# Seven block products for eight in half the contraction of two projection groups

## The chip, the cores and the metric

The kernel runs on one core of a Trainium2 chip. The metric is the device time of one execution in microseconds. TensorE (PE in the profile) multiplies, VectorE (DVE), ScalarE (ACT) and GpSimd (POOL) do the rest, SyncE (SP) and POOL issue the transfers.

## The reference

One step of a hybrid decoder layer: 512 prompt tokens and 8 sample tokens, width 2048. One input projection of the layer input is cut by columns into groups. Three branches run on them: an mLSTM with 4 heads of width 256 (groups mq, mk, mv, output gate mo), a causal depthwise convolution of width 31 on 512 channels with a LayerNorm behind it (cu, cg), and sliding-window attention with 8 query heads (aq, ak, av). Each branch is multiplied by a SiLU gate of its own (mz, cz, az); the results are put side by side and go through an output projection, a residual and a LayerNorm.

```python
mq, mk, mv, mo, mi, mf, mz, cu, cg, cz, aq, ak, av, az = in_projection(x, w_in)
...
m_out = hn * jax.nn.sigmoid(mo.astype(f32)) * jax.nn.silu(mz.astype(f32))
c_out, new_buf = conformer_conv(cu, cg, conv_buf, conv_w, conv_b, conv_ln_g, conv_ln_b)
merged = jnp.concatenate([m_out.astype(x.dtype),
                          (c_out * jax.nn.silu(cz)).astype(x.dtype),
                          (a_out * jax.nn.silu(az)).astype(x.dtype)], axis=-1)
y = jnp.einsum('bte,ed->btd', merged, w_out)
```

## The kernel before

**Tiles of the projection.** The 520 tokens (512 and 8) stand in the free dimension, cut into two halves of 260 columns (`HS`, `hf` 0 and 1). The contraction of 2048 is 16 blocks of 128 (`k`). `ORDER` lists 62 output tiles of 128 columns: ak, av, four aq, for each head two mq, mk and mv, then cg and cu in turn, eight mo, eight mz, four az, four cz. The main loop goes over them; `e` is the number of a tile.

**Split numbers.** Each 32-bit operand is held as a high part in TensorE's format and a low part, the rest. `split` makes them: a cast on ScalarE (line 137) and a subtraction on VectorE (line 138). `mm3` multiplies high by high, low by high and high by low, three matmuls (lines 195 to 197). So one output tile has 16 x 2 x 3 = 96 matmuls of 128x260. The input x is split once and stays (`xh`, `xl`).

**Weights.** A tile's weights come as two halves of 1024 columns, 8 blocks each, in the order of `stream`. `w_load` issues the transfers on SP into one of `NRAW` raw buffers, `w_split` splits them into one of three buffer pairs (`whi`, `wlo`), most of a tile ahead of their use.

**The other work.** Convolution, attention and mLSTM are generators in a queue. After every 24 matmuls (a quarter of a tile, one tick) `pump` gives the queue a budget of credits (`BUDGET` 1.8 up to cg, `BUDGET2` 1.6 from there) and lets the first two generators run until the credits are spent; a step that yields `WAIT` goes on one tick later. `drain` runs a generator to its end. The instructions of TensorE, VectorE and ScalarE run in the order in which the program writes them; those of SP and POOL are ordered by the scheduler of the tile framework. `conv_taps` does 31 taps on VectorE for each of 4 channel blocks, `conv_norm` normalises by token blocks: `fwd` transposes on TensorE, takes statistics and subtracts on VectorE with a power on POOL in between, `bwd` transposes back two ticks later.

**After a tile.** `post_gate` (lines 802 to 805) activates the gate on ScalarE and multiplies it into the merged branch on VectorE. When a merged block is complete, `turn` splits it for the output projection: turns 0 to 7 write into L tiles, 8 to 15 into x tiles. `TURNED` says after which quarter of the cz tiles each is done.

**Buffers.** L, M and S tiles of 1072, 520 and 264 columns come from pools of `NL` 14, `NM` 13 and `NS` 17. A tile takes whichever buffer of its pool is free. In the attention (`att_prompt`), L tiles hold the keys, the queries, the values, the scores of a unit (`scores`) and the two probability tiles of a unit (`flip`); `values` multiplies these one tick after `flip`. PSUM has two pools, 3 banks for the accumulators (`acc_bank`) and 5 for all else (`bank`).

**The end.** Behind the loop, the scale, the bias and the residual are loaded through SP (lines 1040 to 1070). The output projection takes tokens 256 to 519 by output tiles of 128, and `flip_out` adds the residual; then it takes tokens 0 to 255.

## Time and profile before

| what | value |
|---|---|
| median of 3 runs | 1007.62 us (1007.06 to 1007.88) |
| profiled execution | 1005.27 us |
| its span, first to last instruction | 1003.5 us |
| mean granted TensorE clock | 0.997 |
| TensorE busy | 990.5 us |
| VectorE busy | 652.6 us |
| ScalarE busy | 385.4 us |
| POOL busy | 132.8 us |

The time holds the span and some 2 us around it. Busy times are of the profiled execution. TensorE's are pipelined, so that a busy TensorE may be one that waits for its data.

### The profile page before, as it was taken

The page shows a single profiled execution, that of the slowest core. Times are in us where ns is not written, and L with a number is a line of the kernel's source. Part 1 is how long each engine was busy: PE and PEld are TensorE (multiplying, and loading weights), DVE is VectorE, ACT ScalarE, POOL GpSimd, SP SyncE. Part 2 cuts the span into 40 slices and gives each one's busy share as a digit, 9 for nine tenths or more (in the row PEclk, how much of TensorE's full clock was granted, in tenths as well). Part 3 has the DMA queues.
Part 4 walks back from the last instruction along what each step waited for, and adds up shares of the span by engine and source line. Part 5 has one row for each costly group of instructions (what it writes and reads, how often), then busy time and mean ns, then how long its engine had stood idle before and what let it go on. Part 6 is the DMA issues. An engine that isn't in the chain of part 4 may idle for free.

```text
span 1003.5 us, 19258 instructions
## 1 busy us (share of the span) xinstructions
PE 990.5 (99%) x7911; PEld 971.1 (97%) x7911; DVE 652.6 (65%) x1308; ACT 385.4 (38%) x709; POOL 132.8 (13%) x225
## 2 busy tenths in 40 slices
PE   9999999999999999999999999999999999999995
PEld 9999999999999999999999999999999999998885
DVE  6465677567657646765667777778654455558866
ACT  6453454334344334434442222222244443433530
POOL 0010001222222232323311000000000000001102
PEclk9999999999999999999999999999999999999998
DMA  9222214466456436545543323323235585556842
GB/s 333 99 73 97 64 64 131 135 217 192 121 169 188 147 107 221 178 128 154 181 153 102 104 90 104 91 85 102 94 93 169 164 297 170 178 180 205 266 139 84
DMA packets 45976, 147.25 MB, mean 147 GB/s; under 512 B 6749, under 2 KB 8165, under 8 KB 45888
## 3 DMA queue, kind: packets, MB, share of 16 engines
q1 hardware_dynamic: 33840, 110.45, 33.8%
q0 software_dynamic: 11616, 35.03, 11.6%
q8 instruction: 62, 1.02, 0.4%
q10 hardware_dynamic: 432, 0.53, 0.2%
q14 instruction: 26, 0.21, 0.1%
HBM read 130.43 MB, written 15.56 MB: 145 GB/s over the span
## 4 chain that ended last, share of the span: by engine, by line
PE 94%; DVE 3%; ACT 1%; issue 1%; DMA 0%; POOL 0%; SPq 0%; POOLq 0%; DVEq 0%
PE mm L195 27%; PE mm L196 27%; PE mm L197 27%; PE bg L197 2%; PE bg L195 2%; PE bg L196 2%; PE bg L868 1%; PE bg L670 1%; PE bg L484 1%; PE bg L625 0%; DMA wr<-in_w_in 0%; DVE L L427 0%; PE bg L460 0%; PE bg L461 0%; ACT wh L137 0%
## 5 line engine op out<-in xcount | busy, mean ns | idle before, releaser
L195 PE MATMUL mm<-xh,wh 128*128 128x260 f32 (+1 forms) x2096 | 598.1, 285 | 0.5 <-ACT xh L137 0.3
L197 PE MATMUL mm<-xl,wh 128*128 128x260 f32 (+1 forms) x2096 | 592.8, 283 | 0.0
L196 PE MATMUL mm<-xh,wl 128*128 128x260 f32 (+1 forms) x2096 | 592.6, 283 | 0.0
L195 PEld LDWEIGHTS mm<-xh,wh 128*128 128x128 f32 x2096 | 396.0, 189 | 1.8 <-ACT xh L137 0.7
L196 PEld LDWEIGHTS mm<-xh,wl 128*128 128x128 f32 x2096 | 395.4, 189 | 0.7 <-DVE wl L138 0.4
L197 PEld LDWEIGHTS mm<-xl,wh 128*128 128x128 f32 x2096 | 394.8, 188 | 0.0
L138 DVE TENSOR_TENSOR wl<-wr,wh 128x1024 fp32r<-128x1024 f32 (+2 forms) x187 | 225.0, 1205 | 119.1 <-ACT wh L137 116.8
L137 ACT CAST wh<-wr 128x1024 fp32r<-128x1024 f32 (+2 forms) x187 | 193.6, 1035 | 213.3 <-PE mm L197 135.2
L333 DVE SCALAR_TENSOR_TENSOR L<-L,cst 128x512 f32<-128x512 f32 x120 | 90.0, 750 | 2.7
L208 POOL TENSOR_TENSOR T<-T,mhalf 128x1 f32<-128x1 f32 (+1 forms) x30 | 19.3, 645 | 319.5 <-DVE T L206 319.4
L804 ACT ACTIVATE S<-mm 128x260 f32<-128x260 f32 x48 | 18.6, 387 | 97.3 <-PE mm L197 97.3
L805 DVE TENSOR_TENSOR L<-L,S 128x260 f32<-128x260 f32 x48 | 20.6, 430 | 50.3 <-ACT S L804 50.3
L602 ACT ACTIVATE L<-mm 128x260 f32<-128x260 f32 x48 | 18.5, 385 | 64.8 <-PE mm L197 64.5
L195 PE MATMUL mm<-L,wh 128*128 128x264 f32 x128 | 36.4, 285 | 0.0
L196 PE MATMUL mm<-L,wl 128*128 128x264 f32 x128 | 36.4, 284 | 0.0
L197 PE MATMUL mm<-L,wh 128*128 128x264 f32 x128 | 36.3, 284 | 0.0
L777 DVE SCALAR_TENSOR_TENSOR M<-M,T,M 128x256 f32<-128x256 f32 x64 | 30.7, 480 | 6.7 <-ACT M L774 6.7
L780 DVE CUSTOM_DVE_ANT_0 S<-M,M 128x256 f32<-128x256 f32 x64 | 27.2, 425 | 2.2
L783 POOL DMA_DIRECT2D out_Cs<-M x28 | 15.6, 558 | 92.4 <-issue 63.9
L195 PEld LDWEIGHTS mm<-L,wh 128*128 128x128 f32 x128 | 24.1, 188 | 0.0
L197 PEld LDWEIGHTS mm<-L,wh 128*128 128x128 f32 x128 | 24.1, 188 | 0.0
L196 PEld LDWEIGHTS mm<-L,wl 128*128 128x128 f32 x128 | 24.1, 188 | 0.0
(353 smaller groups left out, 1133.1 us busy)
## 6 DMA issues: line engine op xcount, KB each, us to landing
wr<-in_w_in SPq DMA_DIRECT2D x122, 512.0 KB, 3.4
wr<-in_w_out SPq DMA_DIRECT2D x60, 512.0 KB, 3.6
M<-in_C POOLq DMA_DIRECT2D x32, 256.0 KB, 4.5
M<-qkD POOLq DMA_DIRECT2D x32, 256.0 KB, 5.0
out_Cs<-M POOLq DMA_DIRECT2D x32, 256.0 KB, 2.4
M<-in_xT SPq DMA_DIRECT2D x14, 260.0 KB, 6.2
M<-rowsD POOLq DMA_DIRECT2D x8, 260.0 KB, 4.6
M<-in_xp SPq DMA_DIRECT2D x8, 256.0 KB, 5.6
```

Source lines behind the costliest of these rows:

```text
L137: S.copy(out=hi, in_=raw)
L138: V.tensor_tensor(out=lo, in0=raw, in1=hi.bitcast(F32), op=ALU.subtract)
L195: PE.matmul(out, lhsT=wh, rhs=h, start=start, stop=False)
L196: PE.matmul(out, lhsT=wl, rhs=h, start=False, stop=False)
L197: PE.matmul(out, lhsT=wh, rhs=l, start=False, stop=stop)
L208: G.tensor_tensor(out=out, in0=out, in1=mhalf[:rows].broadcast_to([rows, n]) if n > 1 else mhalf[:rows], op=ALU.pow)
L333: V.scalar_tensor_tensor(out=y[:, 0:T], in0=t[:, k:k + T], scalar=cw[:, j, k:k + 1], in1=y[:, 0:T], op0=ALU.mult, op1=ALU.add)
L602: S.mul(out=hT[name, h][:, e, HS[hf]], in_=ps[:, 0:HALF], mul=1.0 / 16.0 if name == "mk" else 1.0)
L777: V.scalar_tensor_tensor(out=ce, in0=qkb[:, DK:2 * DK], scalar=gvv[:, e, b:b + 1], in1=ce, op0=ALU.mult, op1=ALU.add)
L780: V.tensor_tensor_reduce(out=junk, in0=ce, in1=qkb[:, 0:DK], scale=1.0, scalar=0.0, op0=ALU.mult, op1=ALU.add, accum_out=hc[:, e, b:b + 1])
L804: S.activation(out=s, in_=ps[:, 0:HALF], func=func)
L805: V.tensor_tensor(out=dst[:, HS[hf]], in0=dst[:, HS[hf]], in1=s, op=ALU.mult)
```

## The change

The eight tiles az and cz are taken in pairs. For blocks 0 to 7 of the contraction, a pair's product is seen as a 2x2 matrix product: two output tiles, two halves of the tokens, two halves of the eight blocks. It is computed with seven block products (Winograd's form of Strassen's algorithm) from sums of x blocks and sums of weight blocks. Blocks 8 to 15 are multiplied as before. A pair is written out by hand in eleven sections of 12 or 24 matmuls (`pair_up`). In detail:

- `x_sums` loads the quarters of x again through POOL, three tiles before the zone, makes four sums for each of four `j` and splits three; `x_sums_last` splits the fourth into the place of x blocks that are no longer wanted. Twelve M tiles hold the results.
- `prep` loads and splits the weights of a pair in six steps: `a` with the four weight sums behind it, `s12`, `s34`, `a'`, half of `b`, `b'`. `a` and `s12` of the next pair are made in sections 7 and 8.
- The seven products are combined on VectorE (`add`); the last combination and gate of a pair (`last`) stand in section 0 of the next one.
- The queue gets `BUDGET3` 1.2 after sections 1, 3, 5 and 7 to 10, `BUDGET2` is 1.8. `TURNED2` places the turns.
- The weights of az and cz are loaded in the order of the pairs. `NL` is 13, `NS` 13. Scale, bias and the residual of tokens 256 to 511 are loaded through POOL.

```diff
-BUDGET, BUDGET2 = 1.8, 1.6
+BUDGET, BUDGET2, BUDGET3 = 1.8, 1.8, 1.2
-NL, NM, NS, NRAW = 14, 13, 17, 3
+NL, NM, NS, NRAW = 13, 13, 13, 3
...
+SUMS = 3
+ZONE_AT = ("az", 0)
...
-TURNED = {(_i // 4, _i // 2 % 2, _i % 2): (_i - 1,) for _i in range(1, 9)}
-TURNED.update({(3, 0, 1): (8, 9, 10, 11), (3, 1, 0): (12, 13, 14), (3, 1, 1): (15,)})
 CONV0 = ORDER.index(("cg", 0))
+ZONE = ORDER.index(ZONE_AT)
+TURNED2 = {("cz", 0): {2: (0,), 4: (1,), 6: (2,), 7: (3,), 8: (4,), 9: (5,), 10: (6,)},
+           ("cz", 2): {1: (7,), 7: (8, 9, 10, 11), 9: (12, 13, 14), 10: (15,)}}
...
-    stream += [A["w_in"][e, hf] for e in range(2, NE) for hf in range(2)]
+    stream += [A["w_in"][e, hf] for e in range(2, ZONE) for hf in range(2)]
+    stream += [A["w_in"][e + a, hf] for e in range(ZONE, NE, 2) for hf in range(2) for a in range(2)]
...
             submit(("m", i // 2), m_prompt(i // 2))
             submit(("m", i // 2), m_sample(i // 2))
+    NJ = 4
+    sums = {}
+    xn1, xt2, xn3, xn4 = ([None] * NJ for _ in range(4))
+    def x_sums():
+        for j in range(NJ):
+            q = [sml()[:, 0:HALF] for _ in range(4)]
+            for i in range(4):
+                G.dma_start(out=q[i], in_=A["xT"][j + NJ * (i // 2)][:, HS[i % 2]])
+            x11, x12, x21, x22 = q
+            yield 0.0
+            yield WAIT
+            V.tensor_tensor(out=x11, in0=x11, in1=x12, op=ALU.subtract)
+            V.tensor_tensor(out=x12, in0=x12, in1=x22, op=ALU.subtract)
+            V.tensor_tensor(out=x22, in0=x22, in1=x11, op=ALU.add)
+            V.tensor_tensor(out=x21, in0=x21, in1=x22, op=ALU.subtract)
+            sums[j] = x11
+            yield 1.6
+            for dst, src in ((xt2, x22), (xn3, x12), (xn4, x21)):
+                t = mid(F32R)
+                dst[j] = t[:, HS[0]], t[:, HS[1]]
+                split(*dst[j], src)
+            yield 1.3
+    def x_sums_last():
+        for j in range(NJ):
+            xn1[j] = xh[j][:, HS[1]], xl[j][:, HS[1]]
+            split(*xn1[j], sums[j])
+    def w_pair():
+        return (wp.tile([P, 8 * P], F32R, tag="whi", bufs=3, name=nm("wh")),
+                wp.tile([P, 8 * P], F32R, tag="wlo", bufs=3, name=nm("wl")))
+    HW = (slice(0, NJ * P), slice(NJ * P, 2 * NJ * P))
+    wz, rz = {}, {}
+    def prep(q, what):
+        if q >= 2 * NE:
+            w_split(q + (1 if what == "a" else 2 if what == "s12" else 0))
+            return
+        w_load(q + 2)
+        t = None
+        if what == "a":
+            a, b = raws.pop(q), raws[q + 1]
+            t = wz[what] = w_pair()
+            split(*t, a)
+            u, v = (wp.tile([P, 8 * P], F32, tag="wsum", bufs=2, name=nm("ws")) for _ in range(2))
+            for out, x, y in ((u[:, HW[1]], b[:, HW[0]], b[:, HW[1]]), (u[:, HW[0]], u[:, HW[1]], a[:, HW[0]]),
+                              (v[:, HW[0]], a[:, HW[0]], b[:, HW[0]]), (v[:, HW[1]], u[:, HW[0]], a[:, HW[1]])):
+                V.tensor_tensor(out=out, in0=x, in1=y, op=ALU.add)
+            rz["s12"], rz["s34"] = u, v
+            w_load(q + 4)
+        elif what in ("s12", "s34"):
+            t = wz[what] = w_pair()
+            split(*t, rz.pop(what))
+        elif what == "b":
+            t = wz[what] = w_pair()
+            split(t[0][:, HW[0]], t[1][:, HW[0]], raws.pop(q + 1)[:, HW[1]])
+            w_load(q + 6)
+        else:
+            t = wz[what] = w_pair()
+            split(*t, raws.pop(q + (2 if what == "a'" else 3)))
+            w_load(q + (5 if what == "a'" else 7))
+            pos[1] = q + 4
+    def gate(src, name, i, hf):
+        dst = merged({"cz": 0, "az": 4, "mz": 8, "mo": 8}[name] + i)
+        s = sml()[:, 0:HALF]
+        S.activation(out=s, in_=src, func=AF.Sigmoid if name == "mo" else AF.Silu)
+        V.tensor_tensor(out=dst[:, HS[hf]], in0=dst[:, HS[hf]], in1=s, op=ALU.mult)
+    def pair_up(e, late):
+        q = 2 * e
+        na, nb = ORDER[e], ORDER[e + 1]
+        before(*na)
+        before(*nb)
+        p1, p6, p5, p7, c11, c12, c21, c22 = (f()[:, 0:HALF] for f in (
+            acc_bank, acc_bank, acc_bank, bank, bank, acc_bank, acc_bank, acc_bank))
+        s1, u2, u3, u4 = (sml()[:, 0:HALF] for _ in range(4))
+        x0 = [(xh[j][:, HS[0]], xl[j][:, HS[0]]) for j in range(2 * NJ)]
+        x22 = [(xh[j][:, HS[1]], xl[j][:, HS[1]]) for j in range(NJ, 2 * NJ)]
+        def times(out, what, off, xs, start, stop):
+            wh, wl = wz[what]
+            for j in range(NJ):
+                ks = slice((off + j) * P, (off + j + 1) * P)
+                mm3(out, wh[:, ks], wl[:, ks], *xs[j], start and j == 0, stop and j == NJ - 1)
+        def rest(out, what, hf, start):
+            wh, wl = wz[what]
+            for k in range(8, NK):
+                ks = slice((k - 8) * P, (k - 7) * P)
+                mm3(out, wh[:, ks], wl[:, ks], xh[k][:, HS[hf]], xl[k][:, HS[hf]], start and k == 8, k == NK - 1)
+        def add(out, x, y, op=ALU.add):
+            V.tensor_tensor(out=out, in0=x, in1=y, op=op)
+        def sec0():
+            times(p1, "a", 0, x0[:NJ], True, True)
+            if late:
+                late.pop()()
+            prep(q, "s34")
+            S.copy(out=s1, in_=p1)
+        def sec1():
+            times(p6, "s12", 0, xt2, True, True)
+            add(u2, s1, p6, ALU.subtract)
+        def sec2():
+            times(p5, "s12", NJ, xn1, True, True)
+            add(u4, u2, p5)
+            prep(q, "a'")
+        def sec3():
+            times(c11, "a", NJ, x0[NJ:], True, False)
+            prep(q, "b")
+        def sec4():
+            times(p7, "s34", 0, xn3, True, True)
+            add(u3, u2, p7, ALU.subtract)
+            add(u2, u4, p7, ALU.subtract)
+        def sec5():
+            times(c12, "s34", NJ, x22, True, False)
+        def sec6():
+            times(c21, "b", 0, xn4, True, False)
+            prep(q, "b'")
+        def sec7():
+            rest(c11, "a'", 0, False)
+            add(s1, s1, c11)
+            gate(s1, *na, 0)
+            prep(q + 4, "a")
+        def sec8():
+            rest(c12, "a'", 1, False)
+            add(u4, u4, c12)
+            gate(u4, *na, 1)
+            prep(q + 4, "s12")
+        def sec9():
+            rest(c21, "b'", 0, False)
+            add(u3, c21, u3, ALU.subtract)
+            gate(u3, *nb, 0)
+        def last():
+            add(u2, c22, u2, ALU.subtract)
+            gate(u2, *nb, 1)
+        def sec10():
+            rest(c22, "b'", 1, True)
+            if e + 2 < NE:
+                late.append(last)
+            else:
+                last()
+        for i, sec in enumerate((sec0, sec1, sec2, sec3, sec4, sec5, sec6, sec7, sec8, sec9, sec10)):
+            sec()
+            if i in (1, 3, 5) or i > 6:
+                pump(BUDGET3)
+            for k in TURNED2.get(na, {}).get(i, ()):
+                turn(k)
     with tc.manual_schedule(engines=MAN):
-        for e in range(2, NE):
+        for e in range(2, ZONE):
             name, i = ORDER[e]
-            w_split(2 * e + 3)
+            if e == ZONE - SUMS:
+                queue.insert(0, ["x", x_sums(), 0])
+            if e == ZONE - 1:
+                drain("x")
+                prep(2 * ZONE, "a")
+            else:
+                w_split(2 * e + 3)
             budget = BUDGET if e < CONV0 else BUDGET2
             before(name, i)
             ps = [None, None]
             for half in range(2):
                 wh, wl = parts[2 * e + half]
-                if half == 1:
+                if half == 1 and e == ZONE - 1:
+                    prep(2 * ZONE, "s12")
+                    x_sums_last()
+                elif half == 1:
                     w_split(2 * e + 4)
                 for hf in range(2):
                     if half == 0:
                         if hf == 1:
                             after(name, i)
                     pump(budget)
-                    if name == "cz":
-                        for k in TURNED.get((i, half, hf), ()):
-                            turn(k)
+        late = []
+        for e in range(ZONE, NE, 2):
+            pair_up(e, late)
     lng, lnb = [big(), big()], [big(), big()]
     for i in range(2):
         for t, n in ((lng, "lng"), (lnb, "lnb")):
-            SP.dma_start(out=t[i][:, 0:1024], in_=A[n][:, i * 1024:(i + 1) * 1024].partition_broadcast(P))
+            G.dma_start(out=t[i][:, 0:1024], in_=A[n][:, i * 1024:(i + 1) * 1024].partition_broadcast(P))
     def norm_out(tiles, sts, acc, n_st):
         mv = tiny()
     rr = [[mid()[:, 0:512] for _ in range(4)] for _ in range(2)]
     for q4 in range(4):
         for a in range(2):
-            SP.dma_start(out=rr[a][q4], in_=A["xp"][c0 + a * P:c0 + (a + 1) * P, q4 * 512:(q4 + 1) * 512])
+            G.dma_start(out=rr[a][q4], in_=A["xp"][c0 + a * P:c0 + (a + 1) * P, q4 * 512:(q4 + 1) * 512])
```

## Rows read from the trace of the kernel before

**Rows 1.** The page, part 1: engine, busy us, share of the span, instructions.
```profile
PE 990.5 (99%) x7911; PEld 971.1 (97%) x7911; DVE 652.6 (65%) x1308; ACT 385.4 (38%) x709; POOL 132.8 (13%) x225
```

**Rows 2.** The waits of TensorE, whole span: us in total, times, longest.
```profile
PE warm L112 <- DVE S L109: 1.1, 1, 1.1
PE mm L195 <- ACT xh L137: 0.3, 1, 0.3
PE mm L195 <- DVE L L427: 0.2, 1, 0.2
```

**Rows 3.** Windows ahead of and in the changed stretch: busy us (instructions), clock, DMA.
```profile
640.00:708.10 68.10, 68.10 (x571) 68.10 (x571) 54.46 (x76) 16.04 (x23) 0.89 (x1) 1.00 0.32 96
708.10:804.40 96.30, 96.30 (x810) 96.05 (x809) 50.98 (x77) 37.19 (x67) 2.73 (x5) 1.00 0.41 129
```

**Rows 4.** Timeline of ScalarE, gates of mz7 and cz3: start, us, [idle before].
```profile
708.32 0.39 ACT L804 ACTIVATE S<-mm 128x260 f32<-128x260 f32 x1 [2.48 <-PE mm L197]
...
804.67 0.39 ACT L804 ACTIVATE S<-mm 128x260 f32<-128x260 f32 x1 [0.90 <-PE mm L197]
```

**Rows 5.** Timeline of VectorE from 639 to 800 us.
```profile
639.86 0.43 DVE L805 TENSOR_TENSOR L<-L,S 128x260 f32<-128x260 f32 x1 [0.98 <-ACT S L804]
640.21 1.53 DVE L333 SCALAR_TENSOR_TENSOR L<-L,cst 128x512 f32<-128x512 f32 x2
641.66 1.22 DVE L138 TENSOR_TENSOR wl<-wr,wh 128x1024 fp32r<-128x1024 f32 x1
642.79 3.11 DVE L333 SCALAR_TENSOR_TENSOR L<-L,cst 128x512 f32<-128x512 f32 x4
...
761.25 0.70 DVE L138 TENSOR_TENSOR L<-L,L 128x520 fp32r<-128x520 f32 x1
...
796.96 2.53 DVE L138 TENSOR_TENSOR xl<-L,xh 128x520 fp32r<-128x520 f32 x4 [1.19 <-ACT xh L137]
```

**Rows 6.** Timeline of ScalarE, a cast of weights and one of a turn.
```profile
708.60 1.05 ACT L137 CAST wh<-wr 128x1024 fp32r<-128x1024 f32 x1
...
767.65 0.62 ACT L137 CAST L<-L 128x520 fp32r<-128x520 f32 x1
```

**Rows 7.** Timeline of VectorE: the last tap, the first normalising step.
```profile
717.70 0.75 DVE L333 SCALAR_TENSOR_TENSOR L<-L,cst 128x512 f32<-128x512 f32 x1
...
723.11 0.70 DVE L203 BATCH_NORM_STATS2 T<-bg 128x6 f32<-128x512 f32 x1 [0.73 <-PE bg L348]
...
724.89 0.81 DVE L355 TENSOR_SCALAR M<-bg,T 128x512 f32<-128x512 f32 x1 [0.68 <-POOL T L208]
```

**Rows 8.** Attention: a wait of POOL; VectorE's scores and scaling; TensorE's value matmul, transposes.
```profile
POOL L L523 <- PE bg L461: 92.9, 1, 92.9
...
131.83 1.28 DVE L462 TENSOR_TENSOR L<-bg,S 128x512 f32<-128x512 f32 x2
137.42 1.23 DVE L476 TENSOR_TENSOR L<-L,T 128x1024 f32<-128x1024 f32 x1
...
134.30 0.39 PE L497 MATMUL bg<-L,L 128*128 128x512 f32 x1
140.73 1.03 PE L484 MATMUL bg<-ident,L 128*128 128x128 f32 x8
```

**Rows 9.** Windows at the end, behind the last matmul; the granted clock is third from last.
```profile
994.00:996.00 2.00, 0.00 (x0) 0.00 (x0) 1.54 (x4) 1.18 (x2) 0.98 (x2) 1.00 0.00 0
996.00:998.00 2.00, 0.00 (x0) 0.00 (x0) 1.97 (x3) 0.63 (x2) 1.92 (x2) 0.61 0.34 131
998.00:1000.00 2.00, 0.00 (x0) 0.00 (x0) 1.93 (x4) 0.00 (x0) 0.37 (x1) 0.50 0.38 138
```

**Rows 10.** Transfers: an issue on SP's queue; a kind of load with its us to landing.
```profile
780.51 0.33 SPq L1043 DMA_DIRECT2D L<-in_lng  x1
...
M<-in_xT ACTq DMA_DIRECT2D x2, 130.0 KB, 2.6
```

## Prediction

> **What bounds the kernel now.** I read the page first. TensorE is busy for 990.5 us of a span of 1003.5, VectorE for 652.6 [rows 1]. A busy TensorE may still be waiting inside its work, so the list of its waits came next: three, 1.6 us in all, at the start [rows 2]. The windows say the same of the stretch that is changed and of the one before it: PE fills both, and VectorE has 51.0 of 96.3 us of work where the change goes, 54.5 of 68.1 ahead of it [rows 3]. So time is won only by fewer matmuls, and every wait that another engine puts into TensorE's stream is paid in full. The zone (az, cz) runs from 708.1 to 804.4: its ends are the gate activations of mz7 and cz3 [rows 4].
>
> **What is removed.** A tile has 16 x 2 x 3 = 96 matmuls, a pair of tiles 192. In the new pair, sections 0 to 6 have 12 each and sections 7 to 10 have 24 each: 180. Four pairs save 48. The tiles ahead of the zone hold 571 matmuls in 68.10 us, 0.1193 us each [rows 3], so the saving is 48 x 0.1193 = 5.7 us. It is sure, because nothing hides TensorE.
> A rule weighed against this: the Trainium skill's page TensorE: Matmul & The Clock Gate, section Back-to-back issue gap, gives columns / 2.4 + 2.5 ns, which for 260 columns is 110.8 ns, an estimate, and a saving of 5.3 us in place of 5.7. The row decides.
>
> **What is added to VectorE and ScalarE.** Durations, alone or in a queue of their own kind: a 1024-column subtract 1.22 (1.13 from start to start), a 520-column one 0.70 (0.61), a 260-column operation 0.43 (0.35), a convolution tap 0.78 [rows 5]; on ScalarE a 1024-column cast 1.05, a 520-column one 0.62, a gate 0.39 [rows 4, 6]. The operations on 512 columns of weights are not in the trace; I take the 520-column row. Per pair VectorE gets 5.5 splits (6.8 us), four weight sums (2.4), eight combinations (3.4) and four gates (1.7): 14.3 us in a pair of 180 x 0.1193 = 21.5. A bare pair fits, but each result is wanted soon, since a section lasts only 1.43 or 2.87 us. The tight place is the passage from one pair to the next. Counted from the end of section 7, VectorE does a gate (done at 1.5), the split of the next pair's first weights (3.3), the four sums (5.6), the next gate (7.0) and the split of the two-block sums (8.6); TensorE wants those after three long sections and a short one, at 10.1. Work of over 1 to 1.5 us put between them becomes a wait of TensorE, and three things are put there.
>
> **First, the entry.** I counted the queue's credits through both programs. For the old one this puts the last tap into the third quarter of az0 and the first normalising step one quarter later, as the trace has it [rows 7]. For the new one, at 1.8, the x sums take places from mz5 on, the last ones are forced at the start of mz7, taps still fill mz7, and the last is in section 1 of az0. From the gate of mz6's second half (done on ScalarE 0.6 us into mz7) VectorE has in its queue: gates 3 x 0.35, eight x sums 2.8, six x splits 2.1, the first weights' split 1.13, four weight sums 2.44, ten taps 7.3, the sums' split 1.13, four splits of the last x sum 1.4: 19.3 us, while mz7 lasts 11.5. It is 8.5 us behind when the zone starts. Section 1 wants the low part of the sums at 1.55 and gets it at 2.8: 1.3 us of wait. Section 4 wants the low part of the third weights at 5.9 + 1.3 and gets it at 9.8: 2.6 us more. Entry: 3.9 us.
>
> **Second, the normalising steps of the convolution.** One forward step takes VectorE 2.6 us with its trip to POOL (723.11 to 725.70) [rows 7]; its back transposes stand on TensorE two pump places later. In the old zone the places were 2.87 us apart on a quiet VectorE. By the credits the new program has forward steps in az0 at sections 5 and 9, in az2 at 1, 5 and 8, the last back step at section 10. Counted from the end of section 7 of az2, VectorE reaches the sums' split at 8.6 as above and ends the forward step behind it at 11.2; TensorE gets to the back transposes after section 8, eight transposes (1.0) and sections 9 and 10, at 9.6: 1.6 us. Section 1 of az2 has the same with 0.8, and section 6 waits 0.2 for a split behind such a step. Together 2.6 us.
>
> **Third, the turns.** cz0 now has four turns in sections 7 to 10, 0.61 us each: 2.4 us in the passage to cz2, which had 0.9 free where the last combination must leave its PSUM bank for section 2. 1.6 us of wait. In the zone: 3.9 + 2.6 + 1.6 = 8.1 us.
>
> **Fourth, one L tile less, far ahead of the zone.** From attention unit 4 on, the keys (2), queries (4), values (1), merged halves (2), mLSTM inputs (2, later 3), two probability tiles and the new score tile make 14. That none is free the trace shows: POOL, idle, could not load the cached keys into an L tile until the last score matmul [rows 8]. With 13 the score tile has to wait for the first probability tile, which the value matmuls free one section later: the addition that ran at 131.83 can start at 134.30 + 0.39 = 134.7, 2.9 us late. Behind it on VectorE stand the maximum, the sums and the scaling (137.42 + 1.23 = 138.65), and the transposes at 140.73 wait for them [rows 8]: 2.1 us are spare, 0.8 us stalls. Three such units (4, 5, 6): 2.5 us. From below: 0, if the freed tile is not the one that VectorE waits for; from above 2.9 x 3 = 8.7, if the spare time is used otherwise.
>
> **Costed at nothing.** S tiles 17 to 13: I count nine alive at most in the old program, and in the new one some eleven with the x quarters. The budget of 1.8 ahead of the zone: VectorE has 54.5 of 68.1 us there [rows 3], one more half microsecond per tick stays under it, and parts are split most of a tile early. The 16 quarter loads of x on POOL: POOL has under 1 us of work from 640 to 708 [rows 3], such a load lands in 2.6 us [rows 10]; without that cover VectorE is later by as much, once. The scale, bias and residual loads moved from SP to POOL: SP issued the first at 780.5 [rows 10]; they now pass no weight load. They wait for M tiles that the x sums hold until section 6 of the last pair, and the first flip wants them two and a half output tiles after the zone, some 14 us. If late, VectorE stops there and with it the weight splits, some 3 us.
>
> **The sum.** -5.7 + 8.1 + 2.5 = +4.9 us. The profiled execution took 1005.27 us, 1.8 us more than its span; it would take 1010.2. The median of the runs, 1007.62, is 2.4 us above that execution, and the same sum gives **1012.5 us**. About 2 us, 0.2%, is what the measurement can tell from no change.
>
> **The rivals.**
> A. Attention is not touched, because the allocator finds another tile: the zone alone, -5.7 + 8.1, 1010.0. For it: the count of 14 rests on lifetimes that the trace shows only through POOL's wait.
> B. Faster: VectorE keeps up. If its short operations in a queue cost 10% less than I take them for, the entry leaves 1.8, the normalising 1.1 and the turns 0.7: 3.6 us of waits, and with attention untouched -5.7 + 3.6 = -2.1; with only the turns left -4.1, that is 1003.5 to 1005.5. It decides where the waits of zone and attention stay together under 3.7 us. Against it: the durations are rows, and 19.3 us of queue in a tile of 11.5 leave no room.
> C. VectorE falls further behind (the quarter loads, late flips, 5% dearer operations: 10.6 us in the zone): -5.7 + 10.6 + 2.5 + 3, 1018.
> D. The pauses lower TensorE's clock. After the last matmul the granted clock is still 1.00 two to four microseconds on, then 0.61 and 0.50 [rows 9]; my longest pause is 2.6 us. If it fell once, two short sections at half clock cost about 3 us: 1015.5. The Trainium skill's page TensorE: Matmul & The Clock Gate, section Why this matters for your kernels, speaks against the change here: it warns of idle gaps between bursts of matmuls, which bring the half clock back. By that rule, the trace agrees only for a pause longer than those I expect.
> E. Nothing to be measured: waits of 4 to 7.5 us in all, 1005.9 to 1009.4.
>
> **How the numbers follow.** Forecast 0.42, A 0.20, B 0.20, C 0.08, D 0.04, E 0.06. A stands at +2.4, just over the bound, so I give 0.12 of it to slower and 0.08 to same. Slower: 0.42 + 0.12 + 0.08 + 0.04 = 0.66; same 0.14; faster 0.20. The range leaves out the faster half of B and most of C: 1004 to 1017. The likeliest case by itself, with the attention term from 1 to 4 and 6 to 9.5 us in the zone, is 1009 to 1015.5.
>
> **What would show it.** PE's list of waits has new entries: in az0 on the subtract of a split, in az2 at the transposes of the convolution, at the start of cz2 on a combination, and near 131 to 165 us on the scaling of the scores. The count of 128x260 matmuls falls by 48 and the zone gets longer than 96.3 us all the same. The forecast is wrong if PE shows waits under 4 us in all, or if 130 to 170 us passes without one.

## The result, and the profile after

| | before | after |
|---|---|---|
| median of 4 runs | 1007.52 us (1007.06 to 1007.88) | 1018.75 us (1018.07 to 1022.06) |
| profiled execution | 1005.27 us | 1018.33 us |
| its span | 1003.5 us | 1016.5 us |

The change makes the kernel slower: ratio 1.0118, interval 1.0096 to 1.0141. The forecast was 1012.5, slower, with a range that ended at 1017. The direction was right, and the loss is more than twice the one forecast: 11.2 us by the medians, 13.0 by the spans of the profiled executions (that of the kernel before took 2 us less than the runs of this table; run 5 below, beside other runs of the old kernel, gives 13.4 by the medians).

Part 1 of the new kernel's profile page answers to [rows 1]: VectorE has 40 us more work, TensorE 1.3 us less, in a span that is 13.0 us longer.

```profile
PE 989.2 (97%) x7863; PEld 967.1 (95%) x7863; DVE 692.5 (68%) x1396; ACT 400.4 (39%) x739; POOL 145.9 (14%) x253
```

The list of TensorE's waits over the whole span answers to [rows 2] (us in total, times, longest):

```profile
PE mm L203 <- ACT xh L144: 3.3, 2, 1.7
PE mm L204 <- DVE wl L145: 2.3, 1, 2.3
PE bg L204 <- DVE wl L145: 2.3, 1, 2.3
PE bg L372 <- DVE M L363: 2.3, 2, 1.6
PE bg L492 <- DVE L L484: 1.6, 2, 0.8
PE mm L203 <- DVE S L1122: 1.2, 2, 0.9
...
PE bg L492 <- ACT wh L144: 0.8, 1, 0.8
...
PE mm L205 <- DVE xl L145: 0.2, 1, 0.2
```

Nearly every entry that the forecast named is there. The two waits on the low part `wl` are sections 1 and 4 of az0 (L203 to L205 are the lines of `mm3`, L145 the subtract of `split`). The two on `M` are back transposes of the convolution. The two on L1122, the line of `add`, are sections 1 and 2 of cz2. The three at L492 are the flips of attention; one of them is listed under a cast of weights, which ends at the same moment as the scaling (142.07). One entry was not named: of the two waits on the cast `xh`, one is at the start of the program, and the other, 1.7 us, lies behind the zone.

How much TensorE lost is not in that list. It is read from the number of matmuls that it does in a stretch. These windows of the kernel before cover the start and attention (busy us of PE with its instructions, then PEld, DVE, ACT, POOL):

```profile
0.00:130.00 130.00, 128.39 (x1035) 126.95 (x1036) 77.36 (x153) 67.56 (x144) 6.63 (x19) 1.00 0.38 129
130.00:190.00 60.00, 60.00 (x489) 59.11 (x488) 42.08 (x88) 28.56 (x73) 7.96 (x12) 1.00 0.41 127
```

The same of the new kernel, then its zone, whose 100.7 us answer to the 96.30 of [rows 3], and the entry of the output projection:

```profile
0.00:130.00 130.00, 127.05 (x1030) 125.88 (x1031) 76.53 (x153) 67.24 (x144) 6.62 (x19) 1.00 0.38 129
130.00:190.00 60.00, 57.36 (x460) 55.46 (x459) 40.97 (x87) 27.22 (x71) 7.96 (x12) 1.00 0.37 115
712.20:812.90 100.70, 92.58 (x762) 90.84 (x761) 77.04 (x133) 43.50 (x81) 8.64 (x16) 1.00 0.37 121
...
820.00:822.00 2.00, 1.52 (x7) 1.31 (x8) 0.70 (x1) 0.74 (x4) 0.00 (x0) 0.80 0.89 229
822.00:824.00 2.00, 2.00 (x11) 2.00 (x10) 1.12 (x1) 0.85 (x1) 0.00 (x0) 0.50 0.93 261
824.00:826.00 2.00, 2.00 (x16) 2.00 (x15) 0.11 (x1) 0.09 (x1) 0.00 (x0) 0.85 0.98 348
```

In the 60 us of attention 29 matmuls are missing, 3.5 us at 0.12 each, where PE shows 2.64 us of idle time. The zone has 48 matmuls fewer than before and lasts 4.4 us longer. Behind it TensorE pauses from 818.6 to 820.3, and then the granted clock falls from 1.00 to 0.50: 11 matmuls pass in a window that holds 19 at full clock (shown below for run 8).

Two markers tell how late the new kernel is behind that. The first is the first matmul of the output projection, with 264 columns, on TensorE's timeline; the second is ScalarE's copy of the second output tile, which waits for TensorE. Before:

```profile
804.47 0.29 PE L195 MATMUL mm<-L,wh 128*128 128x264 f32 x1
```

```profile
816.35 0.37 ACT L1151 COPY S<-mm 128x256 f32<-128x256 f32 x1 [1.88 <-PE mm L197]
```

After:

```profile
812.91 0.30 PE L203 MATMUL mm<-L,wh 128*128 128x264 f32 x1
```

```profile
828.78 0.37 ACT L1339 COPY S<-mm 128x256 f32<-128x256 f32 x1 [1.82 <-PE mm L205]
```

So the delay is 0.6 us after the first 130 us (five matmuls), 4.1 after attention, 8.4 at the end of the zone, 12.4 after two output tiles and 13.0 at the end. The parts are 0.6 + 3.5 + 4.4 + 4.0 + 0.5, rounded. The 0.6 is a first load of weights that lands later (ScalarE's cast of them starts at 6.78 in place of 5.97); in the experiments below, whose programs are alike there, the same place comes between 0.2 us earlier and 0.6 later than in the kernel before.

The 4.0 behind the zone were in no term of the forecast. TensorE's timeline at the pause, in the last block of the first output tile:

```profile
818.29 0.28 PE L205 MATMUL mm<-xl,wh 128*128 128x264 f32 x1
820.25 0.39 PE L203 MATMUL mm<-xh,wh 128*128 128x264 f32 x1 [1.68 <-ACT xh L144]
820.48 0.28 PE L204 MATMUL mm<-xh,wl 128*128 128x264 f32 x1
820.99 0.44 PE L205 MATMUL mm<-xl,wh 128*128 128x264 f32 x1 [0.22 <-DVE xl L145]
821.23 0.42 PE L203 MATMUL mm<-L,wh 128*128 128x264 f32 x1
821.45 0.42 PE L204 MATMUL mm<-L,wl 128*128 128x264 f32 x1
```

The block that is late is that of turn 15, the last of the zone. Two things are to be seen. From one matmul to the next the pause takes 820.25 - 818.29 = 1.96 us, 1.84 more than 0.12, and the step behind it takes 0.23 in place of 0.12: a listed idle of 1.68 costs about 1.95. And from 821.23 on the matmuls start 0.22 apart, at half clock.

VectorE's timeline says why turn 15 is late (L145 writing `xl` is a turn, `wl` an output weight, L1122 a combination, L1096 the product with a gate):

```profile
808.58 2.52 DVE L145 TENSOR_TENSOR xl<-L,xh 128x520 fp32r<-128x520 f32 x4
...
815.48 0.42 DVE L1096 TENSOR_TENSOR L<-L,S 128x260 f32<-128x260 f32 x1
815.82 1.91 DVE L145 TENSOR_TENSOR xl<-L,xh 128x520 fp32r<-128x520 f32 x3
817.65 0.42 DVE L1122 TENSOR_TENSOR S<-mm,S 128x260 f32<-128x260 f32 x1
817.99 1.21 DVE L145 TENSOR_TENSOR wl<-wr,wh 128x1024 fp32r<-128x1024 f32 x1
819.12 0.42 DVE L1096 TENSOR_TENSOR L<-L,S 128x260 f32<-128x260 f32 x1
```

TensorE left the last section at 812.9; VectorE combines its result at 817.65, behind the turns 8 to 11 (808.58) and 12 to 14 (815.82). Another output weight (817.99) stands between that and the gate of turn 15.

### The profile page after: what moved, and what is told of

Read it like the earlier page. It is cut to its first block, busy times and chain, and to the rows that moved or that the text cites. A ratio compares the mean times of both kernels' runs of the same rounds, so it can differ in the third digit from the quotient of the medians.

```text
span 1016.5 us, 19331 instructions
## 1 busy us (share of the span) xinstructions
PE 989.2 (97%) x7863; PEld 967.1 (95%) x7863; DVE 692.5 (68%) x1396; ACT 400.4 (39%) x739; POOL 145.9 (14%) x253
## 5 line engine op out<-in xcount | busy, mean ns | idle before, releaser
L203 PE MATMUL mm<-xh,wh 128*128 128x260 f32 (+1 forms) x1984 | 566.1, 285 | 4.4 <-ACT xh L144 3.3
L205 PE MATMUL mm<-xl,wh 128*128 128x260 f32 (+1 forms) x1984 | 560.9, 283 | 0.2 <-DVE xl L145 0.2
L204 PE MATMUL mm<-xh,wl 128*128 128x260 f32 (+1 forms) x1984 | 560.7, 283 | 0.0
L203 PEld LDWEIGHTS mm<-xh,wh 128*128 128x128 f32 x1984 | 374.7, 189 | 5.8 <-ACT xh L144 3.8
L204 PEld LDWEIGHTS mm<-xh,wl 128*128 128x128 f32 x1984 | 373.9, 188 | 0.7 <-DVE wl L145 0.4
L205 PEld LDWEIGHTS mm<-xl,wh 128*128 128x128 f32 x1984 | 373.4, 188 | 0.5 <-DVE xl L145 0.4
L145 DVE TENSOR_TENSOR wl<-wr,wh 128x1024 fp32r<-128x1024 f32 (+2 forms) x187 | 222.3, 1192 | 107.5 <-ACT wh L144 106.7
L205 PE MATMUL mm<-L,wh 128*128 128x264 f32 x128 | 37.2, 290 | 0.0
L203 PE MATMUL mm<-L,wh 128*128 128x264 f32 x128 | 37.1, 290 | 0.0
L812 ACT ACTIVATE S<-mm 128x260 f32<-128x260 f32 x32 | 12.3, 386 | 60.8 <-PE mm L205 60.8
L813 DVE TENSOR_TENSOR L<-L,S 128x260 f32<-128x260 f32 x32 | 13.7, 429 | 22.1 <-ACT S L812 22.1
L203 PEld LDWEIGHTS mm<-L,wh 128*128 128x128 f32 x128 | 24.9, 195 | 0.0
L205 PEld LDWEIGHTS mm<-L,wh 128*128 128x128 f32 x128 | 24.8, 194 | 0.0
```

What stands on the lines that cost most here:

```text
L145: V.tensor_tensor(out=lo, in0=raw, in1=hi.bitcast(F32), op=ALU.subtract)
L203: PE.matmul(out, lhsT=wh, rhs=h, start=start, stop=False)
L204: PE.matmul(out, lhsT=wl, rhs=h, start=False, stop=False)
L205: PE.matmul(out, lhsT=wh, rhs=l, start=False, stop=stop)
L813: V.tensor_tensor(out=dst[:, HS[hf]], in0=dst[:, HS[hf]], in1=s, op=ALU.mult)
```

## The experiments

**1. The old kernel with one L tile less.**

```diff
-NL, NM, NS, NRAW = 14, 13, 17, 3
+NL, NM, NS, NRAW = 13, 13, 17, 3
```

> The old kernel with 13 L tiles in place of 14 and nothing else changed. Theory (one L tile less holds up the score tile of attention units 4, 5 and 6): TensorE shows three waits of about 0.8 us each on the scaling of the scores between 140 and 170 us, and the time rises by 2.5 to 3.2 us, to 1010.0 to 1010.8. Rival (the attention waits come from another part of the change, the S tiles or the order of the program): no new wait there, 1007.5 within 1 us.

Median 1010.04 (1009.50 to 1010.43) beside 1006.04 for the old kernel, ratio 1.0041, interval 1.0026 to 1.0056. Its list of waits and its window of attention:

```profile
PE bg L484 <- DVE L L476: 1.6, 2, 0.8
...
PE bg L484 <- ACT wh L137: 0.8, 1, 0.8
PE bg L497 <- DVE L L138: 0.4, 1, 0.4
```

```profile
130.00:190.00 60.00, 57.27 (x459) 55.33 (x458) 40.92 (x87) 27.20 (x71) 7.94 (x12) 1.00 0.36 114
```

The three waits ahead of the flips are there, without anything else of the change, and a short one behind them. The cost is higher than expected: 4.0 us by the medians, and 30 matmuls missing, 3.6 us.

**2. The new kernel with 14 L tiles, paid for with S tiles.**

```diff
-NL, NM, NS, NRAW = 13, 13, 13, 3
+NL, NM, NS, NRAW = 14, 13, 9, 3
```

> The new kernel with 14 L tiles; to make room for it, 9 S tiles in place of 13. Theory: the three waits of attention vanish, 2.5 to 3.2 us less than the new kernel, 1015.5 to 1016.3, and the waits in the zone stay as they are. Rival 1 (the attention waits are not due to the L tiles): 1018.7. Rival 2 (nine S tiles are too few): new waits on S tiles, 1018 or more.

1020.35 (1017.42 to 1021.37), ratio 1.0134 (1.0117 to 1.0151), not faster than the new kernel. The attention waits are gone, but nine S tiles are too few (rival 2). Its list has a new wait:

```profile
PE mm L203 <- ACT S L812: 1.7, 1, 1.7
```

It is on the gate of mz7 (L812), at 711.6, at the head of the zone. Ahead of it VectorE waits 1.75 us for a quarter of x (`S<-in_xT`, at 703.4), a wait that the new kernel doesn't have. The granted clock fell behind three pauses of this execution (at 712, 767 and 821). So the run doesn't price the L tile; run 1 does.

**3. The convolution and the x sums earlier.**

```diff
-BUDGET, BUDGET2, BUDGET3 = 1.8, 1.8, 1.2
+BUDGET, BUDGET2, BUDGET3 = 1.8, 2.2, 1.2
...
-SUMS = 3
+SUMS = 5
```

> The new kernel with a budget of 2.2 in place of 1.8 from cg to the zone and the x sums five tiles ahead of the zone in place of three, so that by the count of credits the convolution ends in mz6 and no tap stands in mz7 or az0. Theory (VectorE's queue at the entry and the normalising steps cause the waits there): the two waits of 2.3 us in az0 and the two of 2.3 us in all at the transposes of the convolution vanish, with about 0.25 us that each hides; 7.5 to 8.5 us less than the new kernel, 1010 to 1011.5; the waits at the start of cz2 and at the entry of the output projection stay. Rival (the zone's own work on VectorE causes them: splits, sums and combinations come too late by themselves): waits of 1 us or more stay in az0 sections 1 and 4, and the time falls by less than 4 us. Second rival (VectorE is overloaded in mo and mz at 2.2): new waits of TensorE between 530 and 700 us on the splits of weights.

1012.34 (1010.64 to 1014.00), ratio 1.0064 (1.0049 to 1.0079), 5.4 to 7.0 us less than the new kernel, by its ratios of 1.0118 above and 1.0134 in run 5. The waits on `wl` in az0 and at the transposes are all gone; those of cz2 and of turn 15 stay:

```profile
PE bg L633 <- DVE M L708: 2.9, 1, 2.9
...
PE mm L203 <- DVE S L1122: 1.2, 2, 0.9
```

The theory of the entry holds: the taps, the x sums and the normalising steps made those waits, and the zone's own work alone makes none there. The gain is less than expected, because the budget of 2.2 already from cg on brings a new wait of 2.9 us at 505, in the mLSTM, and the clock is 0.60 and 0.54 in the two windows behind it. That the splits would wait there was the second rival's; it was another instruction.

**4. The turns of cz2 earlier.**

```diff
-           ("cz", 2): {1: (7,), 7: (8, 9, 10, 11), 9: (12, 13, 14), 10: (15,)}}
+           ("cz", 2): {1: (7,), 3: (8,), 4: (9,), 5: (10,), 6: (11,), 7: (12, 13), 9: (14,), 10: (15,)}}
```

> The new kernel with the turns 8 to 14 of the last pair moved: 8 to 11 from section 7 to sections 3 to 6, 12 and 13 from section 9 to 7, 14 stays in 9, 15 in 10. Theory (these turns make VectorE some 5 us late at the end of the zone, so that turn 15 is late for the first tile of the output projection, and the pause lowers the clock): the wait of 1.7 us near 820 us vanishes and the granted clock stays at 1.00 there; 3.5 to 4.2 us less than the new kernel, 1014.6 to 1015.3. Rival (the fall of the clock is not caused by this pause): the wait vanishes, the clock still falls, 1.9 us less, 1016.8. Second rival (VectorE is late for the splits of the output weights alone): the wait stays at over 1 us.

1014.81 (1013.50 to 1017.02), ratio 1.0091 (1.0076 to 1.0106). The pause behind the zone is gone, and the clock stays at 1.00 there. The second output tile's copy is at 823.96, 7.6 us later than before, and the first matmul of the output projection is also 7.6 late: the 4.0 us between these two markers are back in full. By the ratios the run is 2.7 to 4.3 us under the new kernel; its executions lie 3.5 us apart, and the profiled one lost clock behind the first wait of az0.

**5. The new kernel once more.**

> The new kernel once more, unchanged, beside the two that follow. Theory (each pause of TensorE of some 1.6 us or more lowers the granted clock in some executions and not in others, for some 1.8 us each time): the executions spread over 3 to 4 us where the old kernel's spread over 1, and the ratio to the old kernel is 1.010 to 1.014. Rival (the clock falls only at the entry of the output projection, always there): the executions agree within 1 us.

1018.88 (1017.89 to 1020.05), ratio 1.0134 (1.0119 to 1.0150), beside 1005.52. The executions spread over 2.2 us, less than the 3 to 4 expected; those of the old kernel beside them, but for one, over 0.5. Here is the window behind the pause of 2.3 us in section 1 of az0, first of this execution, then of that of the page above:

```profile
716.00:718.00 2.00, 1.51 (x7) 1.51 (x8) 2.00 (x6) 0.00 (x0) 0.00 (x0) 0.58 0.00 0
```

```profile
716.00:718.00 2.00, 1.46 (x12) 1.47 (x13) 2.00 (x6) 0.00 (x0) 0.00 (x0) 1.00 0.00 0
```

It is the same program and the same pause: once the clock falls behind it, once not. So the clock is lost by execution, as expected. This fall cost next to nothing: while TensorE is slower, VectorE catches up, the wait in section 4 is 0.8 us in place of 2.3, and the first matmul of the output projection is at 812.83 in place of 812.91.

**6. The pauses filled with matmuls.**

```diff
-    def mm3(out, wh, wl, h, l, start, stop):
-        PE.matmul(out, lhsT=wh, rhs=h, start=start, stop=False)
+    def mm3(out, wh, wl, h, l, start, stop, again=0):
+        for i in range(1 + again):
+            PE.matmul(out, lhsT=wh, rhs=h, start=start, stop=i < again)
...
+FILL, FILL_OUT = 17, 13
...
-            times(p6, "s12", 0, xt2, True, True)
+            times(p6, "s12", 0, xt2, True, True, FILL if e == ZONE else 0)
...
-            times(p7, "s34", 0, xn3, True, True)
+            times(p7, "s34", 0, xn3, True, True, FILL if e == ZONE else 0)
...
+            if d == 0 and k == NK - 1:
+                spare = bank()
+                for _ in range(FILL_OUT):
+                    PE.matmul(spare[:, 0:n], lhsT=wh[:, ks], rhs=yh[k - 1][:, c0:c0 + n], start=True, stop=True)
```

> The new kernel with TensorE kept at work in its three longest pauses: in sections 1 and 4 of az0 the first matmul is done 18 times in place of once, and ahead of the last block of the first output tile 13 matmuls of 128x264 go into a spare PSUM bank. VectorE's work and the waits for it stay as they are; only the pauses are filled (2.0, 2.0 and 1.6 us of matmuls in pauses of about 2.6, 2.5 and 1.9). Theory (the pauses lower the clock): the granted clock stays at 1.00 from 700 to 830 us but perhaps for the unfilled pause of 1.65 us near 767, the median falls by 1.5 to 3 us against the new kernel, and the spread of the executions gets smaller. Rival (the fall of the clock at 820 has another cause, such as the entry of the output projection itself): the clock still falls near 820, and the time is that of the new kernel within 0.7 us.

1016.78 (1016.03 to 1017.76), ratio 1.0111 (1.0097 to 1.0125), 2.1 us under run 5 beside it. Windows behind the first pause and around the one behind the zone:

```profile
714.00:720.00 6.00, 5.73 (x48) 5.52 (x47) 5.93 (x12) 1.66 (x3) 0.00 (x0) 1.00 0.06 23
816.00:826.00 10.00, 9.63 (x77) 9.21 (x76) 6.13 (x9) 4.23 (x7) 0.53 (x1) 1.00 0.93 295
```

The clock is 1.00 in both, to the last matmul. VectorE is as late as before, and matmuls that give nothing make the kernel faster. This profile alone would not show the cause, since runs 8 and 10 below keep their clock behind the same pause unfilled. But the mean granted clock of the four executions is 0.994 to 0.996 here and 0.991 to 0.994 in run 5, and runs 4, 7 and 9 enter the output projection without a pause and without a fall: the pauses lower the clock, and the entry by itself does not. Of the 2.1 us, 0.6 are an earlier start by the two profiled executions (the first matmul of the output projection is at 812.22); from there to the second copy this run takes 2.5 us more than the old kernel, run 5 takes 3.9. The spread is smaller by only 0.4 us.

**7. The new kernel with all four places mended.**

```diff
-BUDGET, BUDGET2, BUDGET3 = 1.8, 1.8, 1.2
+BUDGET, BUDGET2, BUDGET3 = 1.8, 2.3, 1.2
...
-NL, NM, NS, NRAW = 13, 13, 13, 3
+NL, NM, NS, NRAW = 14, 13, 12, 3
...
-SUMS = 3
+SUMS = 5
...
-TURNED2 = {("cz", 0): {2: (0,), 4: (1,), 6: (2,), 7: (3,), 8: (4,), 9: (5,), 10: (6,)},
-           ("cz", 2): {1: (7,), 7: (8, 9, 10, 11), 9: (12, 13, 14), 10: (15,)}}
+TURNED2 = {("az", 0): {3: (0,), 5: (1,)}, ("az", 2): {3: (2,), 5: (3,)},
+           ("cz", 0): {2: (4,), 4: (5,), 5: (6,), 6: (7,)},
+           ("cz", 2): {3: (8,), 4: (9,), 5: (10,), 6: (11,), 7: (12, 13), 9: (14,), 10: (15,)}}
...
-            u, v = (wp.tile([P, 8 * P], F32, tag="wsum", bufs=2, name=nm("ws")) for _ in range(2))
+            u, v = wp.tile([P, 8 * P], F32, tag="wsum", bufs=1, name=nm("ws")), a
...
-            w_load(q + 4)
+            w_load(q + 3)
...
+            if what == "s34":
+                w_load(q + 4)
...
-            budget = BUDGET if e < CONV0 else BUDGET2
+            budget = BUDGET if e < CONV0 + 8 else BUDGET2
```

> The new kernel with four edits: 14 L tiles and 12 S tiles (a pair's second weight sum is made in the place of the raw weights, so that one sum buffer is enough); a budget of 1.8 until cu3 and 2.3 from mo0, with the x sums five tiles ahead of the zone, so that by the count of credits the convolution ends in mz7; the turns 0 to 7 spread over az0, az2 and cz0, none of them behind section 6; the turns of cz2 as in the fourth run. Theory (the saving of 48 matmuls is whole and all that ate it were these waits): no wait of 0.5 us or more between 20 us and the end, the clock at 1.00 to the end, the zone shorter than the old one by 5.0 to 5.7 us, 1000.5 to 1002.5, 0.5 to 0.6% faster than the old kernel. Rival 1 (the zone's own work on VectorE doesn't fit the short sections): waits of 1 to 3 us in all stay in the zone, 1003 to 1005. Rival 2 (VectorE is too full from mo to mz at 2.3): new waits there, 1004 or more.

1000.33 (1000.22 to 1001.07), ratio to the old kernel 0.9948, interval 0.9936 to 0.9961: 5.2 us faster than the old kernel, 18.6 faster than the new one. All its waits of TensorE, its zone, and the first matmul of the output projection:

```profile
PE warm L120 <- DVE S L117: 1.1, 1, 1.1
PE mm L204 <- ACT xh L145: 1.0, 1, 1.0
PE mm L204 <- DVE L L436: 0.2, 1, 0.2
```

```profile
712.75:798.90 86.15, 86.15 (x722) 86.15 (x721) 61.08 (x96) 37.30 (x59) 5.86 (x11) 1.00 0.45 158
```

```profile
798.95 0.29 PE L204 MATMUL mm<-L,wh 128*128 128x264 f32 x1
```

Only waits of the first 80 us are left. The zone takes 86.15 us where the old one took 96.30 [rows 3], but the two are not alike: the old zone also holds 40 transposes of the convolution, which this program does ahead of its zone. The saving is read from the first matmul of the output projection, which has the same work ahead of it but for the 48 matmuls: 798.95 is 5.5 us earlier than before, in an execution that was 0.2 late at 75 us. So the 5.7 are whole. VectorE has 692.6 us of work in the whole span, as in the new kernel, but 61.1 of it in the zone, where the new kernel has 77.0: what was wrong was where that work stood (and the missing L tile), not how much it was.

**8. The turns of cz0 earlier, nothing else.**

```diff
-TURNED2 = {("cz", 0): {2: (0,), 4: (1,), 6: (2,), 7: (3,), 8: (4,), 9: (5,), 10: (6,)},
+TURNED2 = {("cz", 0): {1: (0,), 2: (1,), 3: (2,), 4: (3,), 5: (4,), 6: (5, 6)},
```

> The new kernel with the turns of cz0 moved to sections 1 to 6, so that none stands in sections 7 to 10. Theory (the four turns in sections 7 to 10 of cz0 make the combinations late at the start of cz2): the waits of 0.3 and 0.9 us in sections 1 and 2 of cz2 vanish; 1.2 us by the list, 1.7 with what each pause hides, so 1017.0 to 1017.6 beside 1018.8 for the new kernel, all else as there. Rival (splits and weight sums alone make them late): both waits stay within 0.3 us. Second rival: the waits move to sections 2 to 6 of cz0, where the turns now stand ahead of splits.

1016.15 (1015.45 to 1020.20), ratio 1.0109 (1.0088 to 1.0129). Both waits on `add` are gone, none came for them, and the zone is 1.7 us shorter than the new kernel's (its first output matmul is at 811.26, 1.65 earlier). The pause for turn 15 is still there, 1.7 us, but this execution kept its clock:

```profile
820.00:822.00 2.00, 2.00 (x19) 2.00 (x18) 0.76 (x1) 1.21 (x3) 0.00 (x0) 1.00 0.85 304
```

Its second output tile's copy is at 825.68, 9.3 us later than before, the first output matmul 6.8: this entry costs 2.5 us without a fall of the clock, 4.0 with one. The median is 2.6 us under the new kernel's, more than the 1.2 to 1.7 expected; in the profiled execution the clock that stayed up is worth another 1.5.

**9. The mended kernel with 13 L tiles,** 13 S tiles and two sum buffers, as in the new kernel.

```diff
-NL, NM, NS, NRAW = 14, 13, 12, 3
+NL, NM, NS, NRAW = 13, 13, 13, 3
...
-            u, v = wp.tile([P, 8 * P], F32, tag="wsum", bufs=1, name=nm("ws")), a
+            u, v = (wp.tile([P, 8 * P], F32, tag="wsum", bufs=2, name=nm("ws")) for _ in range(2))
...
-            w_load(q + 3)
+            w_load(q + 4)
...
-            if what == "s34":
-                w_load(q + 4)
```

> The mended kernel of the seventh run with 13 L tiles, 13 S tiles and two sum buffers as in the new kernel. Theory (the parts add up): the attention waits are back, 3.6 us in TensorE's stream as in the first run, 1003.7 to 1004.3. Rival (part of the mending came from the sum made in place or from the fourteenth tile elsewhere): 1001 or less, or over 1005 with waits in the zone.

1005.05 (1003.83 to 1006.59), ratio to the old kernel 0.9994 (0.9984 to 1.0003). The attention waits are back, and with them one more in the output projection, at 955:

```profile
PE mm L206 <- DVE wl L146: 1.0, 1, 1.0
```

So this set of buffers decides between 0.5% faster and no difference. Up to the output projection it is the L tile: the first matmul there is at 802.82, 3.9 us behind run 7, and attention accounts for 3.7 (31 matmuls fewer from 130 to 190 us). The parts add up that far, but not to the end: 4.7 us by the medians where 3.6 were expected. What makes the split at 955 late, the L tile or the other two edits, stays open.

**10. The mended kernel with the late turns of cz2.**

```diff
-           ("cz", 2): {3: (8,), 4: (9,), 5: (10,), 6: (11,), 7: (12, 13), 9: (14,), 10: (15,)}}
+           ("cz", 2): {7: (8, 9, 10, 11), 9: (12, 13, 14), 10: (15,)}}
```

> The mended kernel of the seventh run with the turns 8 to 15 of cz2 back in sections 7, 9 and 10. Theory: the wait of about 1.7 us for turn 15 near 805 us is back and lowers the clock behind it in most executions; 2.0 us without a fall of the clock, 4.0 with one, 1002.3 to 1004.5. Rival (VectorE was late at the end of the zone because of work carried over from further ahead, such as the turns of cz0): the wait is under 0.7 us, 1001 or less.

1003.98 (1002.72 to 1006.42), ratio 0.9981 (0.9972 to 0.9991), 3.7 us above run 7. The pause is back, with the other places mended:

```profile
806.06 0.39 PE L204 MATMUL mm<-xh,wh 128*128 128x264 f32 x1 [1.61 <-ACT xh L145]
```

This profiled execution kept its clock and is the fastest of the ten; the median lies 1.3 us above it.

## Why the prediction was wrong

What it named as signs came: the waits in az0, at the transposes, at the start of cz2 and in attention, 48 matmuls fewer and a zone longer than 96.3 us. The sizes did not add up to the time:

| term, us | forecast | idle in the list | cost |
|---|---|---|---|
| 48 matmuls | -5.7 | | -5.7 (run 7) |
| start | 0 | 1.35 | 0.6 |
| attention | 2.5 | 2.6 | 3.5 |
| waits in the zone | 8.1 | 8.0 | 10.1 (100.7 - 96.3 + 5.7) |
| entry of the output projection | 0 | 1.9 | 4.0 |
| rest | 0 | | 0.5 |
| sum | 4.9 | | 13.0 |

**What is removed** was right, by the row: 0.1193 us each. The formula of the Trainium skill's page TensorE: Matmul & The Clock Gate, section Back-to-back issue gap, gave an estimate of 5.3; the page gives it for the gap of an isolated matmul, and the matmuls here are a stream, each with a load of weights.

**First, the entry:** right places and right cause (run 3), 3.9 forecast, 4.6 listed. The low part of the sums came 4.3 us after the start of the zone and not 2.8, so section 1 waited longer and section 4 less than forecast. One size behind that: the four operations of an x sum, counted at 0.35 each, started 0.46 apart (701.74, 702.20, 702.67, 703.13).

**Second, the normalising steps:** 2.6 forecast, 2.3 listed, at the transposes that it named, gone in run 3.

**Third, the turns of cz0:** 1.6 forecast, 1.2 listed, 1.7 in run 8. That the three add up to 8.1 in the forecast and 8.0 in the list is partly luck: the first was 0.7 too small, the other two together 0.7 too large.

**Fourth, one L tile less:** three waits of 0.8 were forecast and found, and run 1 shows the cause. The chain is the one forecast: the addition that ran at 131.83 [rows 8] now waits for the value matmul (L505) and starts 3.4 us later; 0.6 of that is the late start of the program, and 2.8 stand beside the 2.9 that were forecast.

```profile
135.25 1.29 DVE L470 TENSOR_TENSOR L<-bg,S 128x512 f32<-128x512 f32 x2 [2.81 <-PE bg L505]
```

The step that failed is the sum, in two terms. The larger: it ended the count of VectorE's queue at cz2's start. **The sum has no term for the end of the zone,** where the turns 8 to 14 and the output weights stand ahead of the last combination, and turn 15 behind it. The counting of sections that was done for the passage to the next pair was not done for the passage to the output projection; the runs give 2.5 us for its wait in run 8 and 2.4 in run 10. Behind it the clock fell, for another 1.5 (4.0 - 2.5). That was rival D's mechanism, which got a chance of 0.04. Its argument took the end of the kernel, where the clock was still 1.00 two to four microseconds behind the last matmul [rows 9], for a rule about pauses; run 5 shows that a pause of 1.6 us can do it. One end was too little to go by: over the profiles of this case the clock fell between 2.0 us (run 4) and 5.3 us (run 9) behind the last matmul, which ended at 999.99 and 992.02. First run 4, then run 9:

```profile
1002.00:1004.00 2.00, 0.00 (x0) 0.00 (x0) 1.54 (x4) 1.27 (x2) 0.99 (x2) 0.50 0.00 0
```

```profile
996.00:998.00 2.00, 0.00 (x0) 0.00 (x0) 1.97 (x3) 0.57 (x2) 1.92 (x2) 0.82 0.34 131
```

The Trainium skill's page TensorE: Matmul & The Clock Gate, section Why this matters for your kernels, warns of gaps that bring the half clock back, but speaks of gaps longer than the 1.6 to 2.9 us behind which it fell here; the measurement decides.

The smaller: each wait was priced as the idle time that the list would show. A pause costs TensorE about 0.25 us beyond that (1.95 for 1.68 above), and it has ten of them in attention and the zone, with two more in the zone that are too short for the list (0.34 and 0.41 us from one matmul to the next). That is 1.0 in attention and 2.0 in the zone. With the waits as dear as they were measured, and with the 2.5 at the end, the sum would have been -5.7 + 10.1 + 3.5 + 2.5 = +10.4, or 1018.

Of the other rivals, B (VectorE keeps up) was wrong for the program as it stood, though run 7 shows that it could be had with the same work in another order and one L tile more. C's time was nearly right by other causes: no quarter load was late in a wait of TensorE. What was costed at nothing cost nothing in run 7: the budget ahead of the zone, higher there, and the loads on POOL. Fewer S tiles cost something at nine (run 2), and nothing at twelve (run 7).

Open: the wait at 955 in run 9, the spread of that run, the 0.5 us behind the second output tile, and what decides in one execution whether the clock falls.

## What to carry to other kernels

Where one engine is full, follow the helper's queue through every passage of the changed stretch, the way out as well as the way in: the wait that was left out here was the dearest. Price a wait by the matmuls that are missing from a window, not by the idle time listed, and count a pause of 1.6 us or more as one that may also lose clock. When a change that saves work comes out slower, look at the order of what it added before giving it up, and at the buffers it took from others: the same operations, placed earlier and with the fourteenth L tile back, made this one 0.5% faster than the old kernel, and without that tile it gained nothing (run 9).

## What the runs showed of the hardware

The clock falls to 0.50 behind a pause in some executions of one program and not in others: behind the 2.3 us in section 1 of az0 it fell in runs 4 and 5 and not in the first execution of the new kernel shown above or in run 8; behind the pause for turn 15 (1.6 to 2.1 us) it fell in that execution and in runs 2, 3 and 5, and not in runs 8 and 10. No pause of 1.0 us or less was followed by a fall in these profiles. A kernel with long pauses can spread by that: 3.7 us over ten executions in run 10, 0.9 over five in run 7, which has none. It is not the only cause of a spread: run 9, whose longest pause behind the first loads is 1.0 us, spreads over 2.8. And a fall can be nearly free: where TensorE would wait for VectorE again soon (run 5), the half clock only takes the place of the next wait.
